# Attention's finish in a two-layer hybrid encoder: the value product's two halves copied by ScalarE in two pieces and added on GpSimd

## The chip, the core and the metric

The kernel is one program on one core of a Trainium2 chip. The metric is device time in microseconds. The kernel before was timed at 2998.22 us (median of three runs, 2996.7 to 3005.12).

## What is computed

A two-layer encoder on a 1024 x 1024 input: layer 0 mixes by attention, layer 1 by a Hyena convolution, each followed by a gated convolutional FFN. The change is in layer 0's attention, of which the core is

```
def block(q_blk):
    s = jnp.einsum('bqkgd,bskd->bkgqs', q_blk, k, preferred_element_type=jnp.float32) * scale
    p = jax.nn.softmax(s, axis=-1).astype(v.dtype)
    return jnp.einsum('bkgqs,bskd->bqkgd', p, v)
...
return o @ w_o
```

with 16 heads of 64, four key/value heads, blocks of 128 queries against 1024 keys, all in float32.

## The kernel before

To keep float32 accuracy on fast matmuls, operands are split into a rounded high part and a low rest (`_hi`, `_lo`), and products are made of the parts.

Attention runs in 32 **units** (`u`: key/value head g, query block qb), each over the four heads of the group. For a unit, TensorE (PE) makes four **scores** (`scores`, L708 and L709: four matmuls of 512 columns each, into one of two buffers `s_ps`). VectorE (DVE) takes the row maximum (`nmx`, L716), ScalarE (ACT) the exponential (`p_t`, L726) with its sums. Then, eight times per unit, PE transposes a **group** of four 128x128 pieces into `pt_ps` (L732, a ring of three PSUM buffers, tag "pt"), ACT casts it to `pT_hi` (L737), DVE subtracts to `pT_lo` (L162), and PE multiplies both with the values into `o_ps` (L750, L751; one buffer). The values are stored as [high, low] side by side, so rows 0-63 of `o_ps` hold the high half of the product and rows 64-127 the low half: the two have to be added.

That is done by `finish` at the end of each unit. Step 0 makes 1/sums (L761) and spreads it to `rbs` on GpSimd (POOL, L763). Step 2 copies the halves out of PSUM on ACT (L771). Step 3 adds them on DVE (L773), transposes `rbs` on PE into `rb_ps`, which takes one of the three buffers of tag "pt" (L777), multiplies on DVE (L778), which gives that buffer back, and splits the result on POOL (L780, L781).

POOL has two other jobs in attention. `load_q` issues the DMA of the unit after next but one's queries (L693), behind a wait for PE's last use of the buffer. `mod_step` (a step every nine of the 256 groups, in three rounds of eight steps) multiplies a weight tile by a column and adds it up (L187 or L189, then L190; 128x1024 each). When a round ends, PE sums its result (`mod_fin`, L210).

Each engine runs its queue in order. The order in which the code's instructions stand in each queue is set at build by a list scheduler that works with estimates of its own for durations, so another set of instructions can put all queues of attention in another order.

Of the kernel before, what the change touches and what calls it, by code (L numbers as in the profile page):

```python
# [7 lines left out]
F32 = mybir.dt.float32  # L8
# [6 lines left out]
P = 128  # L15
# [6 lines left out]
HD = 64  # L22
# [93 lines left out]
def tile_kernel(ctx: ExitStack, tc: tile.TileContext, t: dict):  # L116
    nc = tc.nc
    mm = nc.tensor.matmul
    V = nc.vector
    ADD, SUB, MUL = ALU.add, ALU.subtract, ALU.mult  # L120
# [388 lines left out]
    with tc.tile_pool(name="x0", bufs=1) as xp:  # L509
# [7 lines left out]
        def load_ada(k):  # L517
            at = ada_tile()
            for i in (1, 0):
                nc.sync.dma_start(at[:, i], t["ada_t"][i, k])  # L520
            return at
# [33 lines left out]
        for k in range(KT):  # L555
            at = load_ada(k) if k >= ADA0 else ada0[k]
# [127 lines left out]
    at = tc.alloc_tile_pool(name="att", bufs=1)  # L684
# [12 lines left out]
    sums, pts, s_t, pt_t, o_t = {}, {}, {}, {}, {}  # L697
# [55 lines left out]
    fin = {}  # L753

    def finish(u, step):
        if u < 0:
            return
        g, qb = divmod(u, NT)
        if step == 0:
            rinv = at.tile([P, 4], F32, name="rinv", tag="rinv", bufs=2)  # L760
            V.reciprocal(rinv, sums[u])  # L761
            rbs = at.tile([P, 4, HD], F32, name="rbs", tag="rbs", bufs=3)
            nc.gpsimd.tensor_copy(rbs, rinv.unsqueeze(2).to_broadcast([P, 4, HD]))  # L763
            fin["rbs", u] = rbs.rearrange("p (a b) d -> p a (b d)", b=2)
        elif step == 2:
            fin["ol"] = at.tile([P, 2, P], F32, name="o_l", tag="o_l", bufs=2)
            fin["os"] = at.tile([P, 2, P], F32, name="o_s", tag="o_s", bufs=2)
            for lo, nm in ((0, "os"), (HD, "ol")):
                ov = o_t[u][lo:lo + HD, :].rearrange("p (a b q) -> p b a q", b=2, q=P)
                for par in range(2):  # L770
                    nc.scalar.copy(fin[nm][par * HD:(par + 1) * HD], ov[:, par])  # L771
        elif step == 3:
            V.tensor_tensor(fin["os"], fin["os"], fin["ol"], op=ADD)  # L773
            rb = ps.tile([P, 512], F32, name="rb_ps", tag="pt", bufs=3)
            fin["rb"] = rb[:, 0:256].rearrange("p (a q) -> p a q", q=P)
            for hp in range(2):
                nc.tensor.transpose(fin["rb"][:, hp], fin["rbs", u][:, hp], ident)  # L777
            V.tensor_tensor(fin["os"], fin["os"], fin["rb"], op=MUL)  # L778
            dst = [o_[:, 2 * g:2 * g + 2, qb * P:(qb + 1) * P] for o_ in (oht, olt)]
            nc.gpsimd.tensor_copy(dst[0], fin["os"])  # L780
            nc.gpsimd.tensor_tensor(dst[1], fin["os"], dst[0].bitcast(F32), op=SUB)  # L781
# [9 lines left out]
    for n in range(len(steps) + LAG):  # L791
        if n < len(steps):
            if steps[n][1] == 0:
                finish(steps[n][0], 0)
            transp(*steps[n])
            pt_hi(*steps[n])
            pt_lo(*steps[n])
        if n >= LAG:
            u, sb = steps[n - LAG]
            attend(u, sb)  # L800
            if sb == NT - 1:
                finish(u, 2)
                finish(u, 3)
        if n == 246:
            w_o0 = load_split(t["w_o"][0], w0_pool, 1)
        i, k = divmod((n - MOD0) // MODD, KT)
        if (n - MOD0) % MODD == 0 and 0 <= i < 3:
            mod_step(3 + i, ssq, k)
        if (n - MOD0) % MODD == MODD - 3 and k == KT - 1 and -1 <= i < 3:
            mod_fin(0, 3 + i, ssq, lambda: ps.tile([P, 512], F32, name="pt_ps", tag="pt", bufs=3))  # L810
        if n < len(steps):
            u, sb = steps[n]
            if sb < 4 and u + 1 < NU:
                scores(u + 1, sb)
                rowmax(u + 1, sb)
                softexp(u + 1, sb)
# [848 lines left out]
    def half1(a):  # L1665
        return [w[k:k + 2, :, 512:1024].rearrange("a p c -> p a c") for k in (a,) for w in (t["w_out"], wold)]

    w2 = [wt.load(*half1(0))]
    for k in range(KT):
# [4 lines left out]
        if k % 2 and k < 7:  # L1674
            src, lo = half1(k + 1)
# [162 lines left out]
```

## Time and profile before

| | |
|---|---|
| median of three runs | 2998.22 us |
| profiled execution, its own time | 2999.89 us |
| its span | 2998.1 us |
| attention's 32 units | about 222 to 622 us of the span |

The span is what the trace covers; the profiled execution's own time is 1.79 us longer. Below, a **pass** is the time from one `rb_ps` transposition on PE (L777) to the next: 31 of them, 231.89 to 616.62 us. Busy times of PE count a matmul to its modelled end, so matmuls overlap in the rows and their pace is read from their starts.

### The profile page before, as it was taken

To read this page: it belongs to the slowest core of one execution; us is meant where nothing else is said; L and a number is where in the kernel's file an instruction comes from. 1 tells how busy PE (TensorE), PEld (TensorE's weight loads), DVE (VectorE), ACT (ScalarE), POOL (GpSimd) and SP (SyncE) were. 2 spreads that over 40 slices of the span, in tenths; PEclk is the share of its full clock that TensorE was granted. 3 is DMA by queue.
4 is the path that set the end of the run, shared out by engine and by line. 5 is a ranking of instruction groups with operands and counts; after the bars stand their busy time and mean duration, and the time that the engine had idled before them with its cause. 6 is when DMAs were issued, how large, how long until landed. Compare 5 with 4: busy or idle time off the path is not lost.

```text
span 2998.1 us, 36517 instructions
## 1 busy us (share of the span) xinstructions
PE 2834.4 (95%) x13152; PEld 2309.0 (77%) x13152; DVE 2289.6 (76%) x3017; ACT 1228.0 (41%) x1998; POOL 536.2 (18%) x452
## 2 busy tenths in 40 slices
PE   5989999999899999999889999999988999999998
PEld 4867777777677787888677878887866888887887
DVE  7788989856997776997667886788976867667544
ACT  3558888833444333334332232323333433333211
POOL 0064465200322232001000000000000323320000
PEclk9999999999999999999989999999998999999999
DMA  6252222132776423975446664665656222223321
GB/s 230 76 170 57 57 64 64 43 129 71 263 235 229 151 84 115 296 249 170 141 158 205 200 217 156 205 204 190 205 183 223 78 85 84 85 77 129 131 84 57
DMA packets 222040, 438.44 MB, mean 146 GB/s; under 512 B 21826, under 2 KB 116834, under 8 KB 217380
## 3 DMA queue, kind: packets, MB, share of 16 engines
q1 hardware_dynamic: 190052, 406.75, 40.1%
q0 software_dynamic: 31808, 29.37, 4.3%
q8 instruction: 104, 1.70, 0.2%
q14 instruction: 76, 0.62, 0.1%
HBM read 307.05 MB, written 128.99 MB: 145 GB/s over the span
## 4 chain that ended last, share of the span: by engine, by line
PE 72%; DVE 13%; DMA 9%; issue 3%; ACT 2%; POOL 1%; SPq 0%; DVEq 0%; ACTq 0%; POOLq 0%
PE w_ps L919 19%; PE d_ps L181 16%; PE u_ps L1278 6%; PE pt_ps L732 3%; PE wo_y L181 3%; PE ab_ps L1414 2%; PE qkv_mm L181 2%; PE o_ps L750 2%; PE o_ps L751 2%; PE s_ps L708 2%; PE s_ps L709 2%; PE g_ps L283 2%; DMA wld<-wi_raw 1%; PE f_ps L462 1%; PE f_ps L463 1%
## 5 line engine op out<-in xcount | busy, mean ns | idle before, releaser
L162 DVE TENSOR_TENSOR w_lo<-u,w_hi 128x1024 fp32r<-128x1024 f32 x120 | 180.5, 1505 | 62.6 <-ACT w_hi L1006 62.6
L1006 ACT CAST w_hi<-u 128x1024 fp32r<-128x1024 f32 x120 | 125.9, 1050 | 209.7 <-PE w_ps L919 204.1
L162 DVE TENSOR_TENSOR pT_lo<-pt_ps,pT_hi 128x512 fp32r<-128x512 f32 x256 | 167.9, 682 | 47.6 <-ACT pT_hi L737 45.5
L181 PE MATMUL d_ps<-s_lo,wd_hi 128*128 128x512 f32 x608 | 195.2, 390 | 0.0
L181 PE MATMUL d_ps<-s_hi,wd_lo 128*128 128x512 f32 x608 | 193.9, 390 | 0.0
L181 PE MATMUL d_ps<-s_hi,wd_hi 128*128 128x512 f32 x608 | 193.7, 391 | 0.0
L919 PE MATMUL w_ps<-t_h,w_hi 128*128 128x512 f32 x480 | 191.2, 398 | 2.5 <-ACT w_hi L1006 1.3
L919 PE MATMUL w_ps<-t_l,w_hi 128*128 128x512 f32 x480 | 190.5, 397 | 0.0
L919 PE MATMUL w_ps<-t_h,w_lo 128*128 128x512 f32 x480 | 189.1, 395 | 0.6 <-DVE w_lo L162 0.6
L1112 DVE SCALAR_TENSOR_TENSOR xd<-d_ps,mod,xd 128x1024 f32<-128x1024 f32 x104 | 132.8, 1281 | 67.8 <-PE d_ps L181 67.5
L737 ACT CAST pT_hi<-pt_ps 128x512 fp32r<-128x512 f32 x256 | 144.9, 588 | 71.3 <-PE pt_ps L732 64.5
L716 DVE TENSOR_REDUCE nmx<-s_ps 128x1 f32<-128x1024 f32 x128 | 155.6, 1217 | 12.8 <-PE s_ps L709 10.8
L732 PE MATMUL pt_ps<-ident,p_t 128*128 128x128 f32 x1024 | 154.2, 274 | 10.3 <-DVE pT_lo L162 9.3
L732 PEld LDWEIGHTS pt_ps<-ident,p_t 128*128 128x128 f32 x1024 | 126.5, 141 | 45.3 <-DVE pT_lo L162 7.7
L919 PE MATMUL w_ps<-fh_h,w_hi 128*128 128x512 f32 x320 | 127.6, 399 | 19.5 <-ACT w_hi L1006 14.6
L726 ACT ACTIVATE p_t<-s_ps,nmx 128x1024 f32<-128x1024 f32 x128 | 143.7, 1124 | 3.1 <-DVE nmx L716 1.9
L1278 PE MATMUL u_ps<-fh_h,w_lo 128*128 128x512 f32 x384 | 140.3, 421 | 2.2 <-DMA w_lo<-wld 2.2
L1027 POOL TENSOR_TENSOR s<-u 128x512 f32<-128x512 f32 x40 | 53.9, 1347 | 487.6 <-DVE w_lo L162 221.5
L1278 PE MATMUL u_ps<-fh_l,w_hi 128*128 128x512 f32 x384 | 136.3, 418 | 1.8 <-DVE fh_l L239 1.8
L1278 PE MATMUL u_ps<-fh_h,w_hi 128*128 128x512 f32 x384 | 131.4, 416 | 3.4 <-ACT fh_h L238 3.4
L181 PEld LDWEIGHTS d_ps<-s_hi,wd_hi 128*128 128x128 f32 x608 | 113.7, 188 | 24.0 <-issue 0.9
L181 PEld LDWEIGHTS d_ps<-s_lo,wd_hi 128*128 128x128 f32 x608 | 113.7, 188 | 23.2 <-issue 0.4
(394 smaller groups left out, 7686.4 us busy)
## 6 DMA issues: line engine op xcount, KB each, us to landing
u<-in_w_up_dram SPq DMA_DIRECT2D x80, 512.0 KB
w_raw<-in_w_down_dram SPq DMA_DIRECT2D x44, 512.0 KB
sg<-gate SPq DMA_DIRECT2D x40, 512.0 KB
w_raw<-sg SPq DMA_DIRECT2D x40, 512.0 KB
w_raw<-in_ada_w_dram SPq DMA_DIRECT2D x32, 512.0 KB
m_raw<-in_ada_t_dram SPq DMA_DIRECT2D x32, 512.0 KB
ed<-eo SPq DMA_DIRECT2D x64, 256.0 KB
eo<-ed SPq DMA_DIRECT2D x16, 1024.0 KB
```

The costliest lines, as they stand in the source:

```text
L162: V.tensor_tensor(lo, src, hi.bitcast(F32), op=SUB)
L181: mm(out[:, cs], lhsT=a, rhs=b[:, cs], start=start and i == 0, stop=stop and i == 2)
L283: mm(pp[:, HS[hf]], lhsT=(wh, wh, wl)[i][:, ks], rhs=hd[hf][i % 2][k], start=k == 0 and i == 0, stop=k == n - 1 and i == 2)
L708: mm(s_ps[:, cs], lhsT=qg[u][:, i], rhs=kTh[g][:, cs], start=True, stop=False)
L716: V.tensor_reduce(nmx, s_t[u, i], op=ALU.max, axis=AX.X, negate=True)
L726: nc.scalar.activation(p_t, s_ps, AF.Exp, bias=nmx, accum_out=sums[u][:, i:i + 1])
L732: nc.tensor.transpose(tp[:, i * P:(i + 1) * P], pts[u, i][:, sb * P:(sb + 1) * P], ident)
L737: nc.scalar.copy(ph, pt_t[u, sb][0])
L919: mm(out, lhsT=(w[0], w[0], w[1])[i][:, k * P:(k + 1) * P], rhs=b[i % 2][k], start=k == 0 and i == 0, stop=k == 3 and i == 2)
L1006: nc.scalar.copy(w[0], src)
L1112: V.scalar_tensor_tensor(x[dt_], yp, gate[dt_], x[dt_], op0=MUL, op1=ADD)
L1278: mm(yp[:, HS[hf]], lhsT=(wh, wh, wl)[i][:, k * P:(k + 1) * P], rhs=hd[hf][i % 2][k], start=k == 0 and i == 0, stop=k == KT - 1 and i == 2)
```

## The change

In `finish`, step 2: instead of four ACT copies of 64x256 (which also put even and odd heads on the right partitions) there are two of 64x512, `o_0` from rows 0-63 and `o_1` from rows 64-127 of `o_ps`, both to partitions 0-63, with one buffer each. The sum is made on GpSimd, by two additions of 64x256 that read partitions 0-63 and write 0-63 and 64-127 of `o_s`. The DVE addition of 128x256 goes. `rbs` gets two buffers instead of three.

```
         elif step == 2:
-            fin["ol"] = at.tile([P, 2, P], F32, name="o_l", tag="o_l", bufs=2)
             fin["os"] = at.tile([P, 2, P], F32, name="o_s", tag="o_s", bufs=2)
-            for lo, nm in ((0, "os"), (HD, "ol")):
-                ov = o_t[u][lo:lo + HD, :].rearrange("p (a b q) -> p b a q", b=2, q=P)
-                for par in range(2):
-                    nc.scalar.copy(fin[nm][par * HD:(par + 1) * HD], ov[:, par])
+            parts = []
+            for i in range(2):
+                o_i = at.tile([HD, 512], F32, name=f"o_{i}", tag=f"o_{i}", bufs=1)
+                nc.scalar.copy(o_i, o_t[u][i * HD:(i + 1) * HD])
+                parts.append(o_i.rearrange("p (a b q) -> p b a q", b=2, q=P))
+            for par in range(2):
+                nc.gpsimd.tensor_tensor(fin["os"][par * HD:(par + 1) * HD], parts[0][:, par], parts[1][:, par], op=ADD)
         elif step == 3:
-            V.tensor_tensor(fin["os"], fin["os"], fin["ol"], op=ADD)
```

(and `rbs` with `bufs=2` for `bufs=3`). The multiplication is L779 in the changed kernel, L778 before; the transposition of `rbs` L778 and L777.

The scheduler's order changes with it, on all engines of attention. **PE, end of the seventh unit** (`s_ps_2997` is the third score of the unit after, `s_ps_3017` its fourth, `s_ps_3091` the first of the one after that; the left-out rows are the second half of the same score). Before:

```order
L708 MATMUL s_ps_2997<-kTh1_447,q_t_2493 128x512
L709 MATMUL s_ps_2997<-kTl1_451,q_t_2493 128x512
...
L751 MATMUL o_ps_2845<-pT_lo_2906,vst6_463 128x512
L732 MATMUL pt_ps_2952<-ident_60,p_t_2801 128x128
...
L750 MATMUL o_ps_2845<-pT_hi_2919,vst7_464 128x512
L751 MATMUL o_ps_2845<-pT_lo_2921,vst7_464 128x512
L777 MATMUL rb_ps_2970<-ident_60,rbs_2778 128x128 x2
L708 MATMUL s_ps_3017<-kTh1_447,q_t_2493 128x512
L709 MATMUL s_ps_3017<-kTl1_451,q_t_2493 128x512
```

and in the changed kernel:

```order
L708 MATMUL s_ps_2997<-kTh1_447,q_t_2493 128x512
L709 MATMUL s_ps_2997<-kTl1_451,q_t_2493 128x512
...
L708 MATMUL s_ps_3017<-kTh1_447,q_t_2493 128x512
L709 MATMUL s_ps_3017<-kTl1_451,q_t_2493 128x512
...
L750 MATMUL o_ps_2845<-pT_hi_2919,vst7_464 128x512
L751 MATMUL o_ps_2845<-pT_lo_2921,vst7_464 128x512
L778 MATMUL rb_ps_2970<-ident_60,rbs_2778 128x128 x2
L708 MATMUL s_ps_3091<-kTh1_447,q_t_2642 128x512
L709 MATMUL s_ps_3091<-kTl1_451,q_t_2642 128x512
```

The third and fourth scores have moved together, and the score after them, which needs the buffer of the third, follows right behind `rb_ps`: three scores stand where two stood, with two matmuls and `rb_ps` between. In 14 of the passes the score behind `rb_ps` follows two others in this way: in five with nothing but those between, in nine with a group of transpositions as well. It is so in none of the passes before but one (see rows 5).

**DVE, the same unit's multiplication** (`pT_lo_2936` and `pT_lo_2959` are groups of the next unit that PE transposes ahead of `rb_ps_2970`, the others are behind it). Before:

```order
L162 TENSOR_TENSOR pT_lo_2936<-pt_ps_2929,pT_hi_2934 128x512
L162 TENSOR_TENSOR pT_lo_2959<-pt_ps_2952,pT_hi_2957 128x512
L716 TENSOR_REDUCE nmx_3022<-s_ps_3017 128x1
L773 TENSOR_TENSOR o_s_2964<-o_s_2964,o_l_2963 128x256
L778 TENSOR_TENSOR o_s_2964<-o_s_2964,rb_ps_2970 128x256
L162 TENSOR_TENSOR pT_lo_2992<-pt_ps_2985,pT_hi_2990 128x512
```

and in the changed kernel:

```order
L162 TENSOR_TENSOR pT_lo_2959<-pt_ps_2952,pT_hi_2957 128x512
L716 TENSOR_REDUCE nmx_3096<-s_ps_3091 128x1
L761 RECIPROCAL rinv_3074<-sums_2949 128x4
L162 TENSOR_TENSOR pT_lo_2992<-pt_ps_2985,pT_hi_2990 128x512
L162 TENSOR_TENSOR pT_lo_3013<-pt_ps_3006,pT_hi_3011 128x512
L716 TENSOR_REDUCE nmx_3130<-s_ps_3125 128x1
L162 TENSOR_TENSOR pT_lo_3033<-pt_ps_3026,pT_hi_3031 128x512
L162 TENSOR_TENSOR pT_lo_3044<-pt_ps_3037,pT_hi_3042 128x512
L162 TENSOR_TENSOR pT_lo_3055<-pt_ps_3048,pT_hi_3053 128x512
L779 TENSOR_TENSOR o_s_2963<-o_s_2963,rb_ps_2970 128x256
```

The multiplication, and with it the return of the buffer that `rb_ps` holds, now stands five groups later in DVE's queue. Of the 32 units, counted from 0, it stands two to five groups later in 20 (2 to 8, 11 to 17 and 20 to 25, while the rounds of `mod_step` run), and within one group of its old place in the other 12.

**POOL, around the same unit's additions**, in the changed kernel:

```order
L693 DMA q_t_3089<-qd0_82 128x4x128
L189 TENSOR_SCALAR w_raw_3589<-w_raw_3589,csil_69 128x1024
L773 TENSOR_TENSOR o_s_2963<-o_0_2964,o_1_2966 64x256 x2
L190 TENSOR_TENSOR ssq_74<-ssq_74,w_raw_3419 128x1024
L763 COPY rbs_3076<-rinv_3074 128x256
L782 TENSOR_TENSOR ol_1838<-o_s_2814,oh_1837 128x2x128
L781 CAST oh_1837<-o_s_2963 128x2x128
```

The two additions stand behind the issue of the query DMA and one multiplication of `mod_step`; the rest of POOL's work per unit is as before.

## Rows read from the trace of the kernel before

**Rows 1.** The page: its first line, PE's busy time (part 1), and the shares of the chain that ended last by engine (part 4).

```profile
span 2998.1 us, 36517 instructions
PE 2834.4 (95%) x13152; PEld 2309.0 (77%) x13152; DVE 2289.6 (76%) x3017; ACT 1228.0 (41%) x1998; POOL 536.2 (18%) x452
PE 72%; DVE 13%; DMA 9%; issue 3%; ACT 2%; POOL 1%; SPq 0%; DVEq 0%; ACTq 0%; POOLq 0%
```

**Rows 2.** Busy time by stretch: single passes, and last all of attention. Columns: from:to, length, then busy us (count) of PE, PE's weight loads, DVE, ACT, POOL, then the granted clock as a share of full speed, the DMA share, GB/s.

```profile
257.60:272.50 14.90, 12.93 (x67) 10.45 (x66) 12.02 (x14) 8.66 (x17) 11.44 (x8) 0.89 0.31 90
295.57:307.06 11.49, 11.49 (x68) 9.26 (x67) 10.41 (x16) 10.09 (x21) 7.47 (x6) 1.00 0.33 98
307.06:318.86 11.80, 11.80 (x67) 9.21 (x66) 11.25 (x16) 10.12 (x21) 9.07 (x6) 1.00 0.29 70
367.46:382.38 14.92, 12.95 (x68) 10.57 (x66) 12.03 (x14) 8.66 (x17) 11.45 (x9) 0.89 0.33 89
477.56:491.31 13.75, 11.64 (x67) 9.33 (x66) 12.15 (x15) 8.67 (x17) 11.23 (x8) 1.00 0.33 95
525.84:537.64 11.80, 11.80 (x68) 9.21 (x67) 11.26 (x16) 10.13 (x21) 9.09 (x6) 1.00 0.29 71
222.00:622.00 400.00, 382.41 (x2167) 307.56 (x2168) 341.48 (x479) 318.67 (x627) 185.13 (x166) 0.99 0.21 53
```

**Rows 3.** Groups of instructions by line, engine and form in 222 to 622 us: busy us, mean ns of one, idle time of the engine just before and what ended it.

```profile
L737 ACT CAST pT_hi<-pt_ps 128x512 fp32r<-128x512 f32 x256 | 144.9, 588 | 71.3 <-PE pt_ps L732 64.5 <-DMA qd<-q_out 2.5 <-PE o_ps L750 1.5
L190 POOL TENSOR_TENSOR ssq<-ssq,w_raw 128x1024 f32<-128x1024 f32 x21 | 50.1, 2386 | 0.2
L773 DVE TENSOR_TENSOR o_s<-o_s,o_l 128x256 f32<-128x256 f32 x32 | 28.1, 877 | 3.4 <-ACT o_l L771 3.4
L781 POOL TENSOR_TENSOR ol<-o_s,oh 128x256 fp32r<-128x256 f32 x32 | 23.7, 740 | 1.2
L771 ACT COPY o_s<-o_ps 64x256 f32<-64x256 f32 x64 | 23.4, 365 | 6.2 <-PE o_ps L751 4.6 <-POOL w_raw L189 1.2
```

**Rows 4.** Instructions in order of time on POOL, DVE and PE after the first `mod_fin`: start, length, what; in brackets the engine's idle time before and what ended it.

```profile
255.93 2.84 POOL L187 TENSOR_SCALAR ssq<-w_raw,csil 128x1024 f32<-128x1024 f32 x1 [6.03 <-PE pt_ps L210]
258.73 0.82 POOL L693 DMA_DIRECT2D q_t<-qd  x1
259.05 3.21 DVE L773 TENSOR_TENSOR o_s<-o_s,o_l 128x256 f32<-128x256 f32 x1
259.57 2.39 POOL L190 TENSOR_TENSOR ssq<-ssq,w_raw 128x1024 f32<-128x1024 f32 x1
262.91 0.66 PE L732 MATMUL pt_ps<-ident,p_t 128*128 128x128 f32 x4 [1.97 <-DVE pT_lo L162]
```

**Rows 5.** The same view near the end of attention: a score's last matmul, its row maximum, its exponential, and the first matmul of the score that takes its buffer.

```profile
560.88 0.39 PE L709 MATMUL s_ps<-kTl,q_t 128*128 128x512 f32 x1
561.31 1.23 DVE L716 TENSOR_REDUCE nmx<-s_ps 128x1 f32<-128x1024 f32 x1 [1.58 <-PE s_ps L709]
562.57 1.11 ACT L726 ACTIVATE p_t<-s_ps,nmx 128x1024 f32<-128x1024 f32 x1
563.83 0.50 PE L708 MATMUL s_ps<-kTh,q_t 128*128 128x512 f32 x1
```

**Rows 6.** The same view, PE alone, at its pace without waits: a group, the last two matmuls of a unit, `rb_ps`.

```profile
305.92 0.39 PE L751 MATMUL o_ps<-pT_lo,vst 128*128 128x512 f32 x1
306.15 0.60 PE L732 MATMUL pt_ps<-ident,p_t 128*128 128x128 f32 x4
306.50 0.48 PE L750 MATMUL o_ps<-pT_hi,vst 128*128 128x512 f32 x1
307.06 0.38 PE L777 MATMUL rb_ps<-ident,rbs 128*128 128x128 f32 x2
307.19 0.47 PE L708 MATMUL s_ps<-kTh,q_t 128*128 128x512 f32 x1
```

**Rows 7.** The same view: a group's transposition, its cast and its subtraction, each begun as soon as the one before allowed it.

```profile
256.00 0.60 PE L732 MATMUL pt_ps<-ident,p_t 128*128 128x128 f32 x4
256.69 0.58 ACT L737 CAST pT_hi<-pt_ps 128x512 fp32r<-128x512 f32 x1 [0.28 <-PE pt_ps L732]
257.31 0.69 DVE L162 TENSOR_TENSOR pT_lo<-pt_ps,pT_hi 128x512 fp32r<-128x512 f32 x1 [1.28 <-ACT pT_hi L737]
```

**Rows 8.** The same view in a pass without `mod_step`: the first copies, the issue of the query DMA, the addition and the multiplication on DVE.

```profile
353.56 0.74 ACT L771 COPY o_s<-o_ps 64x256 f32<-64x256 f32 x2
354.90 0.79 POOL L693 DMA_DIRECT2D q_t<-qd  x1 [6.61 <-PE s_ps L709]
355.82 0.42 DVE L773 TENSOR_TENSOR o_s<-o_s,o_l 128x256 f32<-128x256 f32 x1
356.27 0.42 DVE L778 TENSOR_TENSOR o_s<-o_s,rb_ps 128x256 f32<-128x256 f32 x1
```

**Rows 9.** The same view at the end of attention: the last unit's first copies, and the first matmul of the output projection that needs the result.

```profile
618.36 0.74 ACT L771 COPY o_s<-o_ps 64x256 f32<-64x256 f32 x2 [1.65 <-PE o_ps L751]
621.07 0.47 PE L181 MATMUL wo_y<-oh,w_hi 128*128 128x512 f32 x1 [3.08 <-DVE o_s L778]
```

**Rows 10.** The same view, PE after the second stall of the kind of rows 4.

```profile
374.12 0.63 PE L708 MATMUL s_ps<-kTh,q_t 128*128 128x512 f32 x1
374.55 0.63 PE L709 MATMUL s_ps<-kTl,q_t 128*128 128x512 f32 x1
```

More of the change, by code (lines that the diff above doesn't have):

```diff
@@ L761, in finish @@
             V.reciprocal(rinv, sums[u])
-            rbs = at.tile([P, 4, HD], F32, name="rbs", tag="rbs", bufs=3)
+            rbs = at.tile([P, 4, HD], F32, name="rbs", tag="rbs", bufs=2)
             nc.gpsimd.tensor_copy(rbs, rinv.unsqueeze(2).to_broadcast([P, 4, HD]))
```

## The prediction

> **What bounds the kernel.** I read the page first: PE is busy 95% of the span, and the chain that ended last lies on PE for 72% of it [rows 1]. Then the stretch the change touches: in attention's 400 us PE is busy 382, DVE 341, ACT 319, POOL 185 [rows 2]. Only what makes PE wait there can show in the time. Single passes tell how close the others run behind. A pass with a `mod_step` that goes well takes 11.49 us, and PE is busy for all of it, with DVE at 10.41 and ACT at 10.09 [rows 2]. Three passes are far worse, 14.90, 14.92 and 13.75 us. Next I looked at what PE waited for in the first of these. DVE's addition in `finish` took 3.21 us there, from 259.05 to 262.26, while POOL issued a DMA and then read two tiles for `mod_step`, until 261.96; the `pT_lo` behind it came late, and PE stood 1.97 us [rows 4]. The same addition takes 0.42 us when POOL is idle [rows 8]; its mean is 877 ns [rows 3]. In two of the three passes the granted clock is also 0.89 [rows 2]: after the second such stall score matmuls start 0.43 us apart [rows 10] instead of 0.23, the lower of the two clock levels (1.2 GHz).
>
> **What goes.** The DVE addition goes, and with it the three long passes: 14.90 + 14.92 + 13.75 - 3 x 11.49 = 9.1 us. In the changed order the additions stand on POOL behind the 2.84 us multiplication and the DMA issue that end at 259.55 [rows 4], so they end at about 261; DVE has two subtractions, a maximum and more to do first and doesn't wait. At least the three waits, 3 x 1.97 = 5.9 us, should go; I take all 9.1. Three further passes of 11.80 us hold a shorter wait of the same kind (DVE busy 11.25 instead of 10.41; first and last of the three in rows 2): 3 x 0.31 = 0.9 us. Apart from these, DVE and ACT work less but gain nothing, since PE is full. ACT's two copies of 64x512 lie between 365 ns (half the columns) and 588 ns (as many columns, all partitions) [rows 3]; at 588 they take 1.18 us instead of 1.51.
>
> **What comes: three scores in a row.** This is the term I did not expect from the diff. In 14 passes PE's changed order has two scores close together before `rb_ps`, and a third right behind it, which needs the buffer of the first. The trace has this chain once: a score's last matmul starts at 560.88, DVE starts the maximum at 561.31 having waited for it, the exponential starts at 562.57, and the score that takes the buffer at 563.83, as soon as it was free: 2.95 us from start to start, with no queueing [rows 5]. At PE's pace (0.23 us for a matmul, 0.35 for a group and 0.09 more for the matmul behind it, 0.13 for `rb_ps` [rows 6]) PE has between these two points its own matmul, four of the second score, two of the value product and `rb_ps`: 7 x 0.23 + 0.13 = 1.74 us. It waits 2.95 - 1.74 = 1.2 us in five passes, and 1.2 - 0.44 = 0.75 in the nine that have a group there too: 6.0 + 6.75 = 12.75 us. Where PE comes late anyway, part of it is hidden; below, nothing is the bound (rival 1).
>
> **A buffer held longer.** In 20 units the multiplication stands two to five groups later, so PE's ring of three has two buffers in the meantime. A group's buffer comes back 2.00 us after its transposition started (256.00 to 257.31 + 0.69 [rows 7]) if ACT and DVE are free. At 11.49 / 8 = 1.44 us a group, two buffers give 2.87 us, 0.87 to spare; a maximum of 1.23 us [rows 5] in front of a subtraction makes it 0.36 late. Two of these in a unit are 0.7 us, 14 us in all; the other bound is nothing, since the wait for the score lets ACT and DVE catch up. I take 0.1 us a unit, 2.0.
>
> **The additions themselves.** The trace has no 64x256 addition on POOL; the nearest is the subtraction of 128x256 at 740 ns [rows 3], so two take 1.48 us, and I see no reason why half the partitions should take less. POOL is free for 11.49 - 7.47 = 4 us of a pass with a `mod_step` [rows 2], so it has room. Where the multiplication was put off, the additions end well before it. In the other 12 units they may be late: the DMA issue ahead ends at 355.69, the additions at 357.17, while DVE comes there at 355.82 [rows 8]. The multiplication then starts 0.9 us later than at 356.27. Behind it stand subtractions that give back PE's buffers; 0.9 us is about what a turn of the ring had to spare above (0.87), so little should arrive: I take 0.1 us each, 1.2; the bounds are 0 and 12 x 0.9 = 10.8. At the end of attention nothing hides them: PE waits 3.08 us for the last unit [rows 9], and two copies (-0.33) and two additions for one (1.48 - 0.42) make this 0.7 us longer.
>
> The Trainium skill (GPSIMD Engine Reference, 4.1 Engine selection) speaks against this part: element-wise additions belong on VectorE, because two-input operations are about twice as slow on GpSimd. By it two additions would take an estimated 4 x 0.42 = 1.68 us instead of 1.48, and the last term 0.9 instead of 0.7; the rows agree (740 against 420 ns). The rule doesn't cover the gain, which comes from DVE no longer having to wait for POOL.
>
> **Sum.** -9.1 - 0.9 + 12.75 + 2.0 + 1.2 + 0.7 = +6.7 us. The profiled execution took 2999.89 us, so 3006.5; it lies 1.7 above the median of the runs, so **3005 us** against 2998.2. Nothing after attention changes but a few neighbours in the queues.
>
> **Rivals.** (1) Faster: no wait for scores. If PE is already late where the scores are issued (by the shorter ring), ACT has finished the exponential when PE arrives, and the 12.75 us shrink towards zero. Then -10.0 + 2.0 + 1.2 + 0.7 = -6 gives 2992, and 2988 with the bounds at nothing. For it: a list scheduler put the scores there because its own estimate had PE waiting. Against it: the order of PE, and rows 5, where the same order did make PE wait. It decides below about 0.3 us of wait a pass. (2) Clearly slower: the clock falls at the new waits. After the waits of rows 4 the two slow passes lost 14.92 - 11.49 - 1.97 = 1.46 us beyond the wait, at the lower level. If each of 14 waits does this, 14 x 1.46 = 20 us come on top: 3025. Against it: the third long pass ran at 1.00 [rows 2], and the new waits are about half as long.
>
> For this second rival the Trainium skill has a case (TensorE: Matmul & The Clock Gate, A second HAM failure mode: psum-queue depth-cycling): a kernel with frequent short idles between groups of matmuls lost throughput to clock changes though its median matmul was at full clock. By it the time would be the 3025 just worked out; whether idles of 1 us do this, no row here shows.
>
> (3) Slower by the ring: it costs its upper bound, 14 us, instead of 2, and DVE's waits for POOL 5 instead of 1: 3021. For it: DVE and ACT are near 90% busy [rows 2]. Against it: the gaps the score waits leave.
>
> **How the numbers follow.** My forecast, 2998 to 3012, has 0.5; rival 1, 2986 to 2996, 0.2; rivals 2 and 3 together, 3012 to 3030, 0.3. About 0.3% (9 us) is what a measurement of this kernel can tell from no change. Half of rival 1 lies below 2989: faster 0.12 with a little for the unforeseen. Two thirds of the forecast and half of rival 1 lie within 9 us: same 0.43. The rest is slower, 0.45. For 8 in 10 the range leaves out the lowest and highest tenth: 2989 to 3023.
>
> **What would show it.** Right: no 3 us instruction on DVE in `finish`; the three long passes near 11.5 to 12.5 us; PE waits named after the exponential (`p_t`) on score matmuls in the 14 passes, 0.7 to 1.2 us each; passes there of 12.2 to 12.7 us. Wrong: PE waiting for POOL's result through `pT_lo`, granted clocks under 0.95 in those passes (rival 2), or passes that stay at 11.5 us (rival 1).

## The result, and the profile after

The changed kernel takes 3008.59 us (median; 3002.25 to 3014.82), the kernel before, timed beside it, 2999.51 (2992.07 to 3006.67): a ratio of 1.0026, interval 1.0018 to 1.0035, 9 us slower. The forecast was 3005, 6.7 us slower. The profiled execution took 3002.36 us with a span of 3000.6.

From the first `rb_ps` on PE to the last it is 391.38 us instead of 384.73: **+6.65 us**; the prediction had +6.0 there and +0.7 behind it. (This **stretch** is used below for every kernel. It comes from one execution each; the times of one kernel spread over some 12 us, so a stretch and a median can differ by several.) The rest of the program differs from one execution to the next: what follows the last `rb_ps` took 2381.5 us before and 2377.4 here, so that these two spans are only 2.5 us apart, and in the kernels below it takes 2368 to 2386. So the stretch is where the change can be read, and the 9 us of the medians hold some 2 us that no trace here accounts for.

The page of the changed kernel, its first line, part 1 and the shares of part 4, as in [rows 1]:

```profile
span 3000.6 us, 36585 instructions
PE 2826.5 (94%) x13152; PEld 2301.2 (77%) x13152; DVE 2268.8 (76%) x2985; ACT 1221.7 (41%) x1934; POOL 582.0 (19%) x516
PE 67%; DVE 14%; DMA 9%; issue 4%; ACT 4%; SPq 0%; POOL 0%; DVEq 0%; ACTq 0%; POOLq 0%
```

DVE lost 20.8 us of work, ACT 6.3, and POOL took on 45.8; PE's share of the chain fell from 72 to 67%. Passes of the changed kernel, with the columns of [rows 2]: the first behind a `mod_fin`, three with a `mod_step`, one without:

```profile
257.37:268.66 11.29, 11.29 (x68) 9.42 (x67) 8.83 (x13) 8.43 (x16) 11.02 (x9) 1.00 0.42 118
268.66:281.67 13.01, 11.79 (x67) 9.27 (x66) 10.90 (x16) 10.36 (x18) 10.55 (x11) 1.00 0.36 101
281.67:294.46 12.79, 12.28 (x67) 9.13 (x66) 10.17 (x15) 10.38 (x20) 11.28 (x9) 1.00 0.21 49
307.66:320.19 12.53, 12.03 (x67) 9.09 (x66) 10.20 (x15) 9.60 (x18) 8.95 (x9) 1.00 0.26 64
333.10:344.59 11.49, 11.49 (x67) 9.37 (x66) 9.26 (x14) 9.10 (x18) 3.00 (x6) 1.00 0.13 25
```

The long passes are gone: 11.29, 11.28 and 11.28 us where 14.90, 14.92 and 13.75 stood [rows 2], 9.7 us less. But the passes with a `mod_step` after each of them, 14 in all, now take 12.5 to 13.4 us; they sum to 180.7 us where they took 162.2. PE is not busy for all of them, and POOL, with 9 to 11 us of work a pass, is not full either.

Inside one such pass, in order of time: a score's last matmul on PE, its row maximum on DVE, the subtractions behind it, and PE from the last matmul of the value product on, with the weight load of the next score:

```profile
305.01 0.40 PE L709 MATMUL s_ps<-kTl,q_t 128*128 128x512 f32 x1
305.44 1.22 DVE L716 TENSOR_REDUCE nmx<-s_ps 128x1 f32<-128x1024 f32 x1 [2.04 <-PE s_ps L709]
306.59 1.28 DVE L162 TENSOR_TENSOR pT_lo<-pt_ps,pT_hi 128x512 fp32r<-128x512 f32 x2
307.32 0.50 PE L751 MATMUL o_ps<-pT_lo,vst 128*128 128x512 f32 x1 [0.76 <-DVE pT_lo L162]
307.96 0.19 PEld L708 LDWEIGHTS s_ps<-kTh,q_t 128*128 128x128 f32 x1 [0.16 <-ACT p_t L726]
```

It is the bunched score of [rows 5] again: 305.01 to 307.96 is 2.95 us, to the hundredth what that chain took, and in all 14 places it is 2.94 to 2.96. Only the wait bears another name. DVE stands 2.04 us for the bunched score with the last group's subtraction queued behind the maximum, so PE waits 0.76 for that subtraction ahead of `rb_ps`, and its next weight load only 0.16 for the exponential behind it. Waits of the changed kernel from 222 to 634 us (total, times, longest):

```profile
DVE nmx L716 <- PE s_ps L709: 30.6, 21, 2.2
PEld pt_ps L732 <- DVE pT_lo L162: 15.9, 31, 3.1
PEld o_ps L751 <- DVE pT_lo L162: 14.1, 21, 1.2
DVE o_s L779 <- POOL o_s L773: 5.1, 6, 3.5
```

DVE's wait for scores was 5.3 us in the kernel before. The second row is another thing than the third: there PE (its weight loads, PEld) waits for a subtraction to give back one of the three buffers of tag "pt", and in the 14 passes most of these waits come while `rb_ps` holds one of the three. The chain through the same pass (307.66 to 320.19), by line, tells it at a glance; a pass that goes well has nothing but PE in this row, as the second fence shows, from the kernel with the late multiplication (below):

```profile
by line: DVE nmx L716 19.6%; ACT p_t L726 16.0%; DVE pT_lo L162 15.3%; issue 14.5%; ACT pT_hi L737 13.4%; PE pt_ps L732 10.6%; ACT o L770 9.3%; PE s_ps L709 3.8%; PE s_ps L708 3.7%; PE o_ps L751 1.9%; ACTq L737 0.1%
```

```profile
by line: PE pt_ps L863 31.1%; PE o_ps L875 18.8%; PE s_ps L708 17.4%; PE o_ps L873 16.5%; PE s_ps L709 16.3%; PE rb_ps L801 1.9%
```

### The profile page after: what moved, and what is told of

Same layout as the page of the kernel before. It is cut to its first block, busy times and chain, and to the rows that moved or that the text cites. A ratio compares the mean times of both kernels' runs of the same rounds, so it can differ in the third digit from the quotient of the medians.

```text
span 3000.6 us, 36585 instructions
## 1 busy us (share of the span) xinstructions
PE 2826.5 (94%) x13152; PEld 2301.2 (77%) x13152; DVE 2268.8 (76%) x2985; ACT 1221.7 (41%) x1934; POOL 582.0 (19%) x516
## 4 chain that ended last, share of the span: by engine, by line
PE 67%; DVE 14%; DMA 9%; issue 4%; ACT 4%; SPq 0%; POOL 0%; DVEq 0%; ACTq 0%; POOLq 0%
PE w_ps L920 19%; PE d_ps L181 16%; PE u_ps L1279 5%; PE wo_y L181 3%; PE pt_ps L732 3%; PE qkv_mm L181 2%; PE ab_ps L1415 2%; PE f_ps L462 2%; PE f_ps L463 2%; PE g_ps L283 2%; PE f_ps L181 1%; DMA wld<-wi_raw 1%; DMA qd<-q_out 1%; PE o_ps L751 1%; DVE prod L1485 1%
## 5 line engine op out<-in xcount | busy, mean ns | idle before, releaser
L732 PE MATMUL pt_ps<-ident,p_t 128*128 128x128 f32 x1024 | 153.6, 274 | 12.7 <-DVE pT_lo L162 10.1
L732 PEld LDWEIGHTS pt_ps<-ident,p_t 128*128 128x128 f32 x1024 | 123.8, 140 | 51.5 <-DVE pT_lo L162 15.9
```

Source lines behind the costliest of these rows:

```text
L732: nc.tensor.transpose(tp[:, i * P:(i + 1) * P], pts[u, i][:, sb * P:(sb + 1) * P], ident)
```

## The experiments

The change brought two things at once: operations, and an order that the scheduler built around them. To part them, the order of every attention instruction on PE, DVE and ACT is written out by hand, one string for each queue, and issued in just this order (POOL's queue stays the scheduler's):

```
+    ORDER = {"P": "...", "D": "...", "A": "..."}
+    with tc.manual_schedule(engines={PE, DVE, Activation}):
+        # emit the next token of each queue whose inputs are there
# PE: R rb_ps, Q a score, T a group's transpositions (tt half), h and l the two value matmuls
# DVE: l pT_lo, N maximum, r reciprocal, M multiplication.  ACT: h pT_hi, E exponential, C copies
old order, a regular pass of PE:   R Q T tthltthl Q hT lT hQ lT hlT hlT hQ lT hl
new order, a slow pass of PE:      R Q T hlhT lQ hT lhT lhT lhT lhT lQ Q T hl
old order, DVE up to M:            llN r llN llN llN M      (two groups of the next unit ahead of M)
```

What they gave, beside the kernel before (384.73 us, about 3000) and the changed one (391.38 us, ratio 1.0026):

| finish | queues of PE and ACT | multiplication | stretch us | median us | ratio (interval) |
|---|---|---|---|---|---|
| old | old | old | 383.87 | 3000.42 | 1.0002 (0.9993 to 1.0011) |
| old | new | new, late | 408.95 | 3019.42 | 1.0061 (1.0047 to 1.0076) |
| new | old | old, early | 413.42 | 3039.87 | 1.0135 (1.0120 to 1.0151) |
| new, the changed kernel's buffers | old | old, early | 406.29 | 3020.54 | 1.0067 (1.0047 to 1.0086) |
| new | even | early | 418.34 | 3039.56 | 1.0138 (1.0123 to 1.0152) |
| new | old | four groups | 390.62 | 2999.99 | 1.0005 (0.9993 to 1.0017) |
| new | old | six groups | 370.49 | 2989.22 | 0.9956 (0.9943 to 0.9969) |
| new | even | six groups | 362.39 | 2975.38 | 0.9920 (0.9902 to 0.9937) |
| new, `rb_ps` copied | old | six groups | 399.68 | 3012.85 | 1.0043 (1.0031 to 1.0056) |
| old | even | old | 383.00 | 2999.68 | 0.9999 (0.9986 to 1.0011) |
| two copies, DVE adds | old | old | 394.53 | 3005.08 | 1.0013 (1.0003 to 1.0022) |
| four copies, GpSimd adds | the scheduler's | the scheduler's | 394.37 | 3013.88 | 1.0038 (1.0012 to 1.0063) |

**The control.** Old finish, old order, written out.

> A control for the two others: the finish of the kernel before and its own order of attention, written out by hand in the same way. Both theories expect the kernel before: a stretch of 384 to 386 us between the first and the last `rb_ps`, a ratio of 0.999 to 1.001. If it is off by more, writing an order out costs something by itself, and the two others are read against this one.

Measured: the same time, and the same passes (11.46 us in the regular ones; 13.74, 14.90 and 13.76 behind `mod_fin`, the first at a granted clock of 1.00 where it had 0.89 in the kernel before). Writing an order out costs nothing.

**Old operations, new order.**

> The finish of the kernel before (four ACT copies, the addition on VectorE), with the attention instructions of TensorE, VectorE and ScalarE written out in the order that the changed kernel has; VectorE's addition is put right ahead of the multiplication. Nothing is left out. Theory A (the order): the bunched scores and the late multiplication come back without the new operations: the stretch between the first and the last `rb_ps` is 390 to 397 us, the time 3004 to 3012, a ratio of 1.002 to 1.004. Theory B (the operations): about the kernel before, 2997 to 3001, a ratio of 0.999 to 1.001.

Measured: 408.95 us, 3019.42: more than expected. Two of its passes:

```profile
273.70:287.00 13.30, 12.09 (x68) 9.31 (x67) 11.64 (x17) 10.67 (x20) 9.19 (x9) 1.00 0.36 99
287.00:300.11 13.11, 12.31 (x67) 9.16 (x66) 10.61 (x16) 10.66 (x22) 9.30 (x7) 1.00 0.24 61
```

They are the changed kernel's 13.01 and 12.79 with 0.3 on top. The new order alone, its late multiplication included, makes the passes slow without one of the new operations. (Some passes also hold the old addition's wait, up to 15.2 us; in the second pass shown the unit's addition took 0.42 us, as when nothing holds it.)

**New operations, old order.**

> The changed finish (two ACT copies, two additions on GpSimd), with every attention instruction of TensorE, VectorE and ScalarE written out by hand in the order that the kernel before has; the multiplication stands two or three groups behind `rb_ps` again. `rbs` has three buffers and `o_s` one. Nothing is left out. Theory A (the order costs the time): the stretch from the first `rb_ps` to the last, 384.7 us before and 391.4 after, keeps the gain of the three passes behind `mod_fin` (9.7 us) and none of the loss: about 375 us, and the time is about 2990, a ratio of 0.997 (0.995 to 0.9985). Theory B (the operations cost it): the multiplication stands early again and now waits for additions that GpSimd does behind `mod_step`'s two instructions (2.85 and 2.39 us); VectorE waits 2 to 5 us in a quarter of the 24 passes that have a `mod_step`, 12 to 24 us in sum: 3000 to 3012, a ratio of 1.000 to 1.004.

Measured: 413.42 us, 3039.87. Theory A, which was mine, falls: taking the new order away makes the changed finish 31 us slower, not 18 faster. Theory B had the mechanism, but too small: DVE waits 59.1 us for POOL's additions (222 to 660 us), not 12 to 24. This run had three buffers of `rbs` and one of `o_s`; with the changed kernel's two and two, nothing else changed:

> The changed finish in the old order once more, but with the buffers of the changed kernel (two of `rbs`, two of `o_s`, where the first run of this order had three and one). Theory B (the early multiplication waits for GpSimd's additions, whatever the buffers): again passes of 14 us and more where there is a `mod_step` and 11.9 where there is none, a stretch of 405 to 420 us from the first `rb_ps` to the last, 3030 to 3042. Rival (the one `o_s` buffer made GpSimd's queue late): passes of 11.3 to 11.8, a stretch of 370 to 385, 2989 to 3000.

Measured: 406.29 us, 3020.54. By the medians half of the loss came with the buffers, by the stretch a quarter (7.1 of 28.7 us); the rest stays. A multiplication on DVE, the unit's copies on ACT, what POOL did ahead of it, and the wait in sum (222 to 640 us):

```profile
289.43 1.18 ACT L789 COPY o<-o_ps 64x512 f32<-64x512 f32 x2
289.80 2.40 POOL L190 TENSOR_TENSOR ssq<-ssq,w_raw 128x1024 f32<-128x1024 f32 x1
292.15 0.74 POOL L809 TENSOR_TENSOR ol<-o_s,oh 128x256 fp32r<-128x256 f32 x1
292.84 0.83 POOL L693 DMA_DIRECT2D q_t<-qd  x1
293.69 1.53 POOL L792 TENSOR_TENSOR o_s<-o,o 64x256 f32<-64x256 f32 x2
295.25 0.42 DVE L806 TENSOR_TENSOR o_s<-o_s,rb_ps 128x256 f32<-128x256 f32 x1 [3.47 <-POOL o_s L792]
DVE o_s L806 <- POOL o_s L792: 49.4, 26, 4.2
```

The additions come behind `mod_step`, a subtraction and a DMA issue; DVE stands 3.47 us, and with it everything that PE needs from DVE. Two passes with `mod_step` and one without:

```profile
273.89:289.17 15.28, 12.21 (x64) 9.68 (x63) 10.30 (x15) 9.56 (x18) 14.99 (x11) 0.89 0.30 86
289.17:303.14 13.97, 11.59 (x67) 9.28 (x66) 9.98 (x15) 9.84 (x19) 13.33 (x11) 1.00 0.34 95
331.34:343.24 11.90, 11.59 (x68) 9.27 (x66) 9.97 (x15) 9.83 (x19) 3.81 (x6) 1.00 0.12 22
```

Part of the loss is the clock: the first of these rows has a granted clock of 0.89, as have four more of the passes with `mod_step` in this kernel, and with one `o_s` it fell to 0.82. Even where POOL is nearly idle the early multiplication costs: 11.90 us against 11.46. Spreading the scores evenly in every pass does not help while it stands early:

> The changed finish, written out in the one order of a pass that the kernel before has in 16 of its passes, in 24 of the 28 from the second on (one score behind `rb_ps`, three more spread over the groups, the multiplication two groups behind `rb_ps`); in the three passes with `mod_fin` its matmuls stand ahead of the last group. Theory A (the order): no pass is worse than 11.5 us, and those of the trains may come to the 11.3 of the changed kernel's passes behind `mod_fin`: 2983 to 2990, a ratio of 0.994 to 0.997. Theory B (the operations): as with the old order, 2998 to 3012.

Measured: 418.34 us, 3039.56, with one `o_s` as in the first run.

**The multiplication alone.** So the late multiplication is what GpSimd's lateness needs, and the question is whether it must come with bunched scores. Here the old order is kept on PE and ACT, and on DVE only the multiplication moves:

```
-DVE, old order, from one unit's M on:   M llN r llN llN llN M ...
+DVE, late, from the same place:         llN r ll M N llN llN ...    (the same unit's M, six groups behind the unit)
```

> The changed finish; TensorE and ScalarE in the old order, so the scores stay spread, but in the first 29 units VectorE's multiplication stands six groups behind its unit instead of two or three; so it no longer waits for GpSimd, and `rb_ps` keeps one of the three buffers for some 5 us longer. Nothing is left out. It parts what the late multiplication takes (the buffer) from what the bunched scores take. Theory A1 (the bunched scores are what the changed kernel pays, the buffer costs little, as in the prediction's two terms, 12.75 and 2.0): the passes with `mod_step` come to 11.5 to 11.8, the stretch from the first `rb_ps` to the last to 376 to 383 us, the time to 2991 to 2998. Theory A2 (the buffer is what is paid; the scheduler bunches the scores because a transposition can't be placed while two buffers are left): the passes stay at 12.3 to 13.2 or more in all 28 units, the stretch is 395 to 415 us, the time 3010 to 3030.

Measured: 370.49 us, 2989.22 us, ratio 0.9956: faster than both kernels. Against the early multiplication with the same buffers, moving one instruction in DVE's string is worth 36 us of stretch. Not all of it is that place by itself: the scheduler, which still orders POOL, answered by putting the additions ahead of `mod_step`'s work in some passes. In the unit shown above they begin 3.08 us after the copies end (293.69 against 290.61), and in the same unit here 1.01 us:

```profile
286.17 1.18 ACT L789 COPY o<-o_ps 64x512 f32<-64x512 f32 x2
288.36 1.57 POOL L792 TENSOR_TENSOR o_s<-o,o 64x256 f32<-64x256 f32 x2
290.03 2.85 POOL L189 TENSOR_SCALAR w_raw<-w_raw,csil 128x1024 f32<-128x1024 f32 x1
```

In the passes without `mod_step`, where the additions end 2.5 us after the copies in both kernels, the place alone makes 11.9 into 11.26 us. A pass behind `mod_fin`, then two with `mod_step`, and two waits (222 to 640 us), DVE's for the additions and PE's for a buffer of tag "pt":

```profile
262.96:274.64 11.68, 11.36 (x67) 9.31 (x66) 8.90 (x13) 8.53 (x16) 11.48 (x9) 1.00 0.38 114
274.64:285.90 11.26, 10.52 (x64) 8.60 (x63) 10.18 (x15) 9.57 (x18) 11.08 (x10) 1.00 0.37 107
308.42:319.68 11.26, 11.26 (x68) 9.33 (x66) 9.98 (x15) 9.84 (x19) 11.08 (x10) 1.00 0.27 71
DVE o_s L806 <- POOL o_s L792: 3.7, 2, 3.5
PEld pt_ps L863 <- DVE pT_lo L162: 4.0, 7, 0.8
```

DVE's wait for POOL is gone but for the end of attention. And `rb_ps` holds one of PE's three buffers for some 7 us of the pass (308.42 to 315.61 in the last row's), at no visible price: no kernel here has a better steady pass than these 11.26 us. Theory A1 stands in its mechanism, and its range (376 to 383) was too cautious: the changed kernel, which has the multiplication as late in the 20 units but the scores bunched, loses 20.9 us of stretch that spread scores give back, and a held buffer alone is not what costs. Whether it adds to the loss while scores are bunched is not shown: the waits for a "pt" buffer are 31 there and 7 here, and no run has bunched scores with an early multiplication. Next, a place between the two:

> As the kernel with the late multiplication, with the multiplication four groups behind its unit instead of six, 2.8 us earlier by passes of 11.26 us for eight groups. If the multiplication's place against GpSimd's additions is what decides, the loss lies between: in the old order the multiplication waited 59 us in 26 passes, 2.3 in the mean and 6.5 at the most, so 2.8 us more leave the longest of these waits: a stretch of 372 to 392 us, 2992 to 3008. If any place behind the additions' usual end will do, it is as with six, 2988 to 2991.

Measured: 390.62 us, 2999.99. DVE's wait falls from 49.4 to

```profile
DVE o_s L806 <- POOL o_s L792: 29.6, 14, 3.6
```

and passes without `mod_step` are already at 11.25, those with it at up to 15.7: 3021, 3000 and 2989 us for two or three, four and six groups. These three are not steps of one thing, because POOL's queue came out differently in each. In the same unit as above the additions now stand behind both instructions of a `mod_step` and begin 4.82 us after the copies end:

```profile
283.08 1.18 ACT L789 COPY o<-o_ps 64x512 f32<-64x512 f32 x2
285.89 2.38 POOL L190 TENSOR_TENSOR ssq<-ssq,w_raw 128x1024 f32<-128x1024 f32 x1
289.08 1.53 POOL L792 TENSOR_TENSOR o_s<-o,o 64x256 f32<-64x256 f32 x2
```

Where nothing holds it, the multiplication at this place starts 2.94 us after the copies; with additions that end 2.6 us after them, as in this unit of the kernel with six groups, it would not have waited. What the runs show is that the multiplication has to stand behind the additions' end, wherever POOL puts that.

**A run that settled nothing.** To test the buffer from the other side, `rb_ps` was copied out at once:

> As the kernel with the late multiplication, but ScalarE copies `rb_ps` into SBUF right behind its two copies of the value product (128x256, some 0.4 us by the copies of 64x512, 0.58), and the multiplication reads the copy: the buffer is free again after some 2 us, and the multiplication may wait for GpSimd without holding TensorE. Theory A1: like the kernel without the copy, less or more 2 us. Theory A2: the passes with `mod_step` come to 11.4 to 11.8, the stretch to 375 to 383 us, the time to 2990 to 2998, and the difference to the kernel without the copy is the price of the held buffer. Either way, if the passes are still above 12.3, the cause is neither.

Measured: 399.68 us, 3012.85, neither of the two. For room this kernel had one `o_s` again, and the late multiplication waited all the same: in the unit shown, its additions on POOL come after the subtraction that frees `o_s`, another `mod_step` and a copy.

```profile
292.33 0.75 POOL L809 TENSOR_TENSOR ol<-o_s,oh 128x256 fp32r<-128x256 f32 x1
296.57 1.53 POOL L792 TENSOR_TENSOR o_s<-o,o 64x256 f32<-64x256 f32 x2
298.14 0.43 DVE L806 TENSOR_TENSOR o_s<-o_s,rb_c 128x256 f32<-128x256 f32 x1 [2.62 <-POOL o_s L792]
```

What the copy by itself would do stays open; the run without it had left it little to gain.

**The halves, and the addition's old place.** The two copies with the additions left on DVE, in the old order:

> Half of the change with the order held: ScalarE's two copies of 64x512 in place of four, but the two shifted additions stay on VectorE, where the addition stood; TensorE, VectorE and ScalarE in the old order. Nothing is left out. If the additions on GpSimd are all of the loss (both the waits of the old order and the new order that avoids them), this is no slower than before: a stretch of 378 to 386 us, 2993 to 3001, a ratio of 0.998 to 1.0005. If the copies cost it, 3003 or more.

Measured: 394.53 us, 3005.08. By the expectation's own rule this speaks against the copies; the rows give the old reason: its passes are 11.28 us where POOL leaves DVE alone, 12 to 15.5 where not, and its additions take 50.1 us of DVE in sum where the single one took 28.1 [rows 3]. The two additions on DVE and POOL's read beside them:

```profile
261.66 3.62 DVE L795 TENSOR_TENSOR o_s<-o,o 64x256 f32<-64x256 f32 x2
262.19 2.37 POOL L190 TENSOR_TENSOR ssq<-ssq,w_raw 128x1024 f32<-128x1024 f32 x1
```

The other half, four copies and one addition on GpSimd, in the scheduler's own order:

> The other half of the change in the order that falls out by itself: four ACT copies as before, and the one addition of 128x256 on GpSimd instead of VectorE. Nothing is left out. In the order of TensorE the multiplication then stands up to nine groups behind its unit and two scores stand right behind one another in half of the passes. Theory (GpSimd's addition, through the order that it brings, is the loss): passes of 12.5 to 14 where the scores are bunched, 3003 to 3020, a ratio of 1.002 to 1.007. Rival (the two copies and their shifted layout bring the order and the loss): no slower than before, 2990 to 3000.

Measured: 394.37 us, 3013.88, with passes of 12.6, 13.4 and 14.7 after each `mod_fin`: the addition on GpSimd brings an order like the changed kernel's without the new copies (the chain of 2.95 us is there in eight passes). And the old finish with even scores:

> The finish of the kernel before, nothing else changed but that 24 of the 28 passes from the second on are written out in the order of its 16 regular passes, with `mod_fin`'s matmuls ahead of the last group of their pass. It asks whether the 14.90, 14.92 and 13.75 us of the passes behind `mod_fin`, which the prediction put down to VectorE's addition, need that addition to go to GpSimd at all. If the addition behind GpSimd's writes is the cause whatever the order: passes of 14 to 15 stay, 2995 to 3001. If it takes the bunched scores of these passes as well: they come to 11.5 to 12.5, the stretch to 375 to 380 us, the time to 2990 to 2995, a ratio of 0.997 to 0.9985.

Measured: 383.00 us, 2999.68. The passes behind `mod_fin` came to 13.57 us only, and others rose to 13.1 and one to 15.8. The addition is held up there with the scores spread, too:

```profile
258.66 3.16 DVE L792 TENSOR_TENSOR o_s<-o_s,o_l 128x256 f32<-128x256 f32 x1
259.15 2.38 POOL L190 TENSOR_TENSOR ssq<-ssq,w_raw 128x1024 f32<-128x1024 f32 x1
```

So in its old place the addition has to leave DVE if this is to be gained. The other way, the old finish with addition and multiplication both late and the scores spread, was not run; so it is not shown that the move to GpSimd is needed for what follows.

**The version that the runs point to:** new finish, late multiplication, even scores.

> The late multiplication (six groups) together with the even order of the scores in all passes from the second to the 29th, `mod_fin`'s matmuls ahead of the last group of their pass. With the old order the late multiplication left 13.97 and 11.66 us for the two passes around each `mod_fin` and 15.28, 13.44, 12.36 and 13.99 for passes 26 to 29; the other passes took 11.26. If spread scores are all that a pass needs, the pairs come to about 13 and 11.3 and passes 26 to 28 to 11.3 to 12: some 3 us and 4 to 8 us less, 2977 to 2984, a ratio of 0.9925 to 0.995. If what is left there is `mod_fin` and the loads of the next stage, 2987 to 2990 as without it.

Measured: 362.39 us, 2975.38 us, ratio 0.9920, better than expected: 24 us below the kernel before, 33 below the changed one. All but seven of the 31 passes take 11.22 to 11.28 us; the pair around the first `mod_fin`:

```profile
247.22:260.23 13.01, 13.01 (x84) 11.12 (x83) 11.03 (x17) 9.89 (x19) 4.51 (x7) 1.00 0.12 22
260.23:271.48 11.25, 11.25 (x67) 9.34 (x66) 9.29 (x13) 9.85 (x19) 10.33 (x8) 1.00 0.44 119
```

## Why the prediction came out right, and where it was wrong

**The addition's wait, -9.1.** Right: -9.7, and at its old place the addition stays slow with the scores spread (above). **The scores, +12.75, the buffer, +2.0, and the short waits that go, -0.9.** Together 13.85; measured 180.7 - 162.2 = 18.5 in the 14 passes with `mod_step`. Of this 3 x 0.92 = 2.8 is a score (four matmuls at 0.23) that the new order moved into three of these passes from others, so 15.7 against 13.85. The chain was sized to the hundredth, 2.95 us, but that the sum came so near is partly luck. The same finish with the scores spread (the kernel with the late multiplication) takes 157.7 us for these 14 passes. Against that the new order costs 180.7 - 157.7 - 2.8 = 20.2 us, where I had 12.75 + 2.0 = 14.75; and the finish without its new order gains 162.2 - 157.7 = 4.5 us, where I had 0.9. Two misses, 5.4 too little loss and 3.6 too little gain, nearly cancel.

The split between scores and buffer stays open: a held buffer alone costs nothing visible, but in the changed kernel part of the loss shows as waits for a buffer of tag "pt" (15.9 us of the weight loads, above). And two signs by which I meant to know the order were wrong. The passes take 12.5 to 13.4 us, not 12.2 to 12.7. The waits of PE are not named after the exponential: in the pass shown that wait is 0.16 us, because it shows one step earlier, at the subtraction behind DVE's maximum. The pass of [rows 5] could have told me so, with 0.52 us for the subtraction and the same 0.16 for the exponential:

```profile
563.19 0.19 PEld L751 LDWEIGHTS o_ps<-pT_lo,vst 128*128 128x128 f32 x1 [0.52 <-DVE pT_lo L162]
563.83 0.19 PEld L708 LDWEIGHTS s_ps<-kTh,q_t 128*128 128x128 f32 x1 [0.16 <-ACT p_t L726]
```

**The additions, +1.2 and +0.7 at the end.** Right in size: DVE waits 5.1 us in all for POOL, 3.5 of it for the last unit, where PE's wait grew from 3.08 [rows 9] to 3.5 us; `L773` takes 732 ns for half of the partitions, as much as 128x256 did [rows 3]. But I called the late multiplication a cost. In the old order, which I held to be the better one, these waits are 49.4 us; the place that I charged with 2.0 is what keeps them at 5.

The Trainium skill's rule that two-input work is about twice as slow on GpSimd (GPSIMD Engine Reference, 4.1 Engine selection) agrees roughly, at 748 ns (the kernel with four copies) against 420 for one addition of 128x256. The two of 64x256 together cost twice that, 2 x 732 ns. The rule does not tell the larger part: when GpSimd gets to it.

**"DVE and ACT work less but gain nothing, since PE is full."** Wrong by 0.2 us in every pass: regular passes were 11.46, and are 11.26 wherever the multiplication is late enough, though PE looked busy for all of the 11.49 [rows 2]. In the kernel before, the last copy of a unit and the next unit's first value matmul, which needs `o_ps`:

```profile
296.60 0.75 ACT L771 COPY o_l<-o_ps 64x256 f32<-64x256 f32 x2
297.40 0.50 PE L750 MATMUL o_ps<-pT_hi,vst 128*128 128x512 f32 x1
```

The matmul starts 0.05 us after the copies end, 0.69 us after the six transpositions before it began (296.71); in the late kernel these take 0.58. Two copies (2 x 0.58 us) free `o_ps` 0.3 us sooner than four (4 x 0.37). That is 0.1 of the 0.2; the other 0.1 was not traced. That the copies bring it, and not the additions, is shown by 11.28 us with the additions on DVE.

**The rivals.** The clock (2): in the changed kernel the granted clock is 1.00 in all 31 passes, so the 20 us did not come; it did fall in the kernels with longer stalls, as with the early multiplication (0.89, above). By the case in the Trainium skill (TensorE: Matmul & The Clock Gate, A second HAM failure mode: psum-queue depth-cycling) they might have; the trace does not show it at waits of 0.8 us in passes of 12.5. The ring at its bound (3): not as a cost of the late multiplication alone, which is nothing; with bunched scores it is part of the open split. No score waits (1), 2992 us: not in the changed kernel, but it is near what the same finish gives, at 2989, once the scores stand where they were.

So the total was near because the order was read from the queues and priced by one row, and because two misses offset each other; that this order was the scheduler's answer to GpSimd's late additions, and that half of the answer (the multiplication) was right and half (the bunched scores, with that late multiplication) a loss of 20 us, only the runs showed.

## What to carry to other kernels

Where a scheduler sets the order, compare operations at a fixed order and orders at fixed operations: here the same finish takes 3040, 3021, 3009, 2989 or 2975 us by order and buffers alone. Work that goes to a slower, shared engine needs distance: move its consumer back in the waiting engine's queue, and give its output a second buffer, before judging the move. And watch the queues that a scheduler still orders: here POOL's changed each time DVE's did. A bunched pair of producers on a full engine showed here as a wait on something else, one instruction further down the consumer's queue; the chain by line of one pass found it where the list of PE's waits did not.

## What the runs showed of the hardware

A two-input DVE instruction on SBUF is held while GpSimd reads two SBUF tiles: the addition that takes 0.42 us alone [rows 8] took 3.16 us beside a GpSimd read of 2.38, and two of 64x256 took 3.62. Each time the held addition ended 0.3 us behind the end of that read. The multiplication, with one input in PSUM, stayed at 0.41 us in the mean. The Trainium skill has this as an exclusive lock on a shared pair of ports (SBUF — State Buffer, SBUF: two separate sides); the rows agree in how the hold ends. They don't show the read to be all of it: the addition began 0.49 us before it (258.66 against 259.15), while POOL issued a query DMA as in [rows 4], and at 0.42 us would have been done by then. Half the partitions do not make a GpSimd addition shorter: 732 ns for 64x256, 748 for 128x256 in the kernel with the four copies.
